# Weight tiles of 512 columns, the next pair's weights issued before this pair's products, three down rounds and 58 Strassen pairs in a two-block network on one core

## The chip, the core and the metric

The kernel runs on one core of a Trainium2 chip. The metric is the time of one execution in microseconds. TensorE (PE) multiplies, VectorE (DVE) and ScalarE (ACT) work on tiles in SBUF and empty PSUM, GpSimd (POOL) does little here, and SyncE (SP) issues nearly all loads.

## The reference

Sequences of 512 tokens with 1024 channels go through two models one after the other, two layers each, all in float32.

```python
for l in range(DEPTH):          # first model
    x = x + rms_norm(mixers(rms_norm(x, ...)) @ w_out[l], norm_mix_post[l])
    h = rms_norm(x, norm_mlp_pre[l])
    y = conv_mlp(h, w_up[l], conv_w[l], conv_b[l], w_down[l])
    x = x + rms_norm(y, norm_mlp_post[l])
# second model: 16 meta tokens are put ahead, 528 tokens
for l in range(DEPTH):
    h = h + 0.5 * swiglu(rmsnorm(h, g0), ffn_w_gate[l, 0], ffn_w_up[l, 0], ffn_w_down[l, 0])
    h = h + mixer(rmsnorm(h, g1), ...)
    h = h + 0.5 * swiglu(rmsnorm(h, g2), ffn_w_gate[l, 1], ffn_w_up[l, 1], ffn_w_down[l, 1])
def swiglu(x, w_gate, w_up, w_down):
    return (jax.nn.silu(x @ w_gate) * (x @ w_up)) @ w_down
```

Gate and up are 1024 x 2816, down is 2816 x 1024. The change touches the four `swiglu` blocks, and every weight load of the program.

## The kernel before

**Products.** Channels lie on partitions, tokens in columns. For float32 accuracy every operand is split into a high part (`whi`, `xh`) that ScalarE rounds and a low part (`wlo`, `xl`) that VectorE subtracts, and each product of 128 x 128 weights is three matmuls: high by high, high by low, low by high (`mm3`, L225 for 512 columns, L233 for halves of 256 and 272).

**Weights.** `wload` takes a tile of up to 1024 columns by a DMA on SP's queue (L191), then `wsplit` makes its high half on ScalarE (L202) and its low half on VectorE (L203). All weight tiles, `raw`, `sum`, `whi` and `wlo`, share 13 buffers of 1024 columns (`NW`).

**A feed-forward block** (`ffn2`) goes through 22 pairs of 128 gate rows and 128 up rows, m = 0 to 21. In a direct pair (m in `DIRECT`, and the first three of the first block) each of the two is a group of its own: 8 chunks of channels x 3 matmuls, in two halves of tokens for 528 tokens, so 48 matmuls a weight (tile `gu`). All other pairs, 66 in the four blocks, are done with seven products in place of eight (`strassen`): the gate's and the up's two halves of channels are a, b, c, d, VectorE makes four sums of weights (`pair`, L1001), and each product is 12 matmuls of 264 columns (256 in the last block, which has 512 tokens), 84 for a pair. They are named here by their weights: a, b, s2, s1, s3, d, s4. Three accumulators in two PSUM tiles (`yx` with Y and X, `z` with Z) are used over again:

```python
self.prod(Y, wg, 0, x1, a, True)        # a
nc.scalar.copy(pv[:, a], Y)             # L1041
self.prod(X, wg, 512, x2, a, True)      # b
tt(s[:, a], X, pv[:, a], ALU.add)       # L1039
self.prod(Y, w12, 512, fv, a, False)    # s2, goes on in Y
nc.scalar.copy(pv[:, b], Y)             # L1046
...
self.prod(Y, w34, 0, fu, b, False)      # s3, goes on in Y
nc.scalar.copy(v3[:, b], Y)             # L1052
```

Product d then goes on in Y, and s4 in Z. `strassen` is a generator: products d and s4 of a pair are emitted between products of the next one. `act` multiplies by the norm (L1091), takes silu (L1092), multiplies gate by up (L1093) and splits (L210, L211).

**Down.** After pair 11 (`NH` - 1) and after pair 21 the activations made so far go through the down weights: 8 outputs, each with 12 or 10 chunks (`dn`), added to the stream `xt` by VectorE (L1137). Two loads of 768 or 640 columns bring the weights of an output.

**Order.** The code is written in a program order. A scheduler with a table of costs then orders the instructions of each engine, with earlier ones first where several can run, and gives out the buffers; the order on each engine is fixed when the program is built. PSUM in this part is three tiles of two banks (`P`). Activations and temporaries use 63 buffers of 528 columns (`NSLOT`).

Of the kernel before, what the change touches and what calls it, by code (L numbers as in the profile page):

```python
# [22 lines left out]
NX = 512  # L23
# [12 lines left out]
NSLOT = 63  # L36
# [13 lines left out]
NW = 13  # L50
NH = 12
DIRECT = (0, 5, 9, 13, 18)
# [7 lines left out]
class Net:  # L60
# [30 lines left out]
    def begin(self, srcs, T, g):  # L91
# [13 lines left out]
        for k in range(0, NK, 2):  # L105
            for w in ws[:1]:
                self.wsplit(*w, slice(128 * k, 128 * k + 256))
            xs.append(self.xsplit(k, g(k), c))
            for w in ws[1:]:
                self.wsplit(*w, slice(128 * k, 128 * k + 256))  # L110
# [75 lines left out]
    def wload(self, src):  # L186
        if self.pre:
            return self.pre.pop(0)
        n = src.shape[-1]
        raw, hi, lo = self.wtiles()  # L190
        self.nc.sync.dma_start(raw[:, :n], src)  # L191
        self.wsplit(raw, hi, lo, slice(0, n))
        return hi, lo

    def wtiles(self):
        return self.wtile("raw", F32), self.wtile("whi"), self.wtile("wlo")

    def wtile(self, n, dt=F32R):
        return self.wp.tile([128, 1024], dt, tag="w", name=self.nm(n), bufs=NW)

# [13 lines left out]
    def mm3(self, ps, w, wc, xs, T, first, last, M=128, halves=(0, 1)):  # L214
# [6 lines left out]
        for i, (a, b) in enumerate(((wh, xh), (wh, xl), (wl, xh))):  # L221
            st, sp = first and i == 0, last and i == 2
            lh = a[:, wc : wc + M]
# [256 lines left out]
    def mixer1(self, l, xs):  # L480
# [441 lines left out]
    def mlp1(self, l, xs, next_g, tn):  # L922
# [22 lines left out]
        for m in range(NF):  # L945
# [27 lines left out]
        srcs = lambda m: [  # L973
            d["w_down"][l, m][:, 1024 * c : min(DFF, 1024 * c + 1024)] for c in range(3)
        ]
        for m in range(NK - 1):
# [4 lines left out]
            [srcs(NK - 1)], [(k // 8, 128 * (k % 8), k) for k in range(NF)], acts, ys, gcol, next_g, tn  # L981
        )

    def down(self, srcs, acts, T, p):
        k = 0
        for src in srcs:
            w = self.wload(src)
            for j in range(src.shape[-1] // 128):
                self.mm3(p[0], w, 128 * j, acts[k], T, k == 0, k == len(acts) - 1)
                k += 1  # L990
# [5 lines left out]
    def pair(self, gsrc, usrc):  # L996
# [3 lines left out]
        A, B = slice(0, 512), slice(512, 1024)  # L1000
        tt = lambda o, i, j, op: nc.vector.tensor_tensor(out=o, in0=i, in1=j, op=op)  # L1001
        wg, wu = self.wtiles(), self.wtiles()
        nc.sync.dma_start(wg[0], gsrc)
        nc.sync.dma_start(wu[0], usrc)
        w12, w34 = ((self.wtile("sum", F32), self.wtile("whi"), self.wtile("wlo")) for _ in range(2))
        g, u, s12, s34 = wg[0], wu[0], w12[0], w34[0]
        tt(s12[:, A], u[:, A], u[:, B], ALU.add)
        tt(s12[:, B], s12[:, A], g[:, A], ALU.subtract)
        tt(s34[:, A], g[:, A], u[:, A], ALU.subtract)
        tt(s34[:, B], g[:, B], s12[:, B], ALU.subtract)  # L1010
        self.wsplit(*wg, slice(0, 1024))
        self.wsplit(*w12, slice(0, 1024))
        self.wsplit(*w34, slice(0, 1024))
        self.wsplit(*wu, B)
        return [w[1:] for w in (wg, wu, w12, w34)]

    def prod(self, o, w, wc, xs, c, first):

        for k in range(NK // 2):
            l = slice(wc + 128 * k, wc + 128 * k + 128)  # L1020
# [6 lines left out]
    def strassen(self, gsrc, usrc, xs, T, rb, act):  # L1027
# [5 lines left out]
        wg, wu, w12, w34 = self.pair(gsrc, usrc)  # L1033
        x1, x2 = xs[: NK // 2], xs[NK // 2 :]
        fu, fv = zip(*self.forms)
        pa, pz = self.P("yx"), None
# [888 lines left out]
```

## Time and profile before

| | |
|---|---|
| median of 3 runs | 3728.61 us (3727.02 to 3731.86) |
| the profiled execution | 3724.06 us |
| its span, first to last instruction | 3722.3 us |
| busy: PE, DVE, ACT | 95%, 63%, 43% |
| mean granted TensorE clock | 0.985 |
| chain that ended last: PE, DVE, ACT, DMA | 80%, 12%, 4%, 3% of the span |

The rows of the profile give an engine's busy time, the count of instructions in brackets, and the idle time before an instruction with what ended it. Matmuls are pipelined, so their own durations overlap; the step from one start to the next tells the pace. The granted clock of 1.00 is the upper of TensorE's two levels, 2.4 GHz. The eight stretches of gate and up pairs begin at 1240, 1469, 2090, 2309, 2491, 2712, 3311 and 3529 us and take 1118 us together; down rounds, two mixers of each model and the convolution blocks fill the rest.

### The profile page before, as it was taken

Reading aid. Unit: us, or ns where it says so; the run is one execution under the profiler, and the core shown is the slowest. Engines: PE = TensorE matmul, PEld = TensorE weight load, DVE = VectorE, ACT = ScalarE, POOL = GpSimd, SP = SyncE. Lnnn points to the kernel's source line nnn. Section 1 sums busy time; section 2 is a strip of 40 time slices with the busy share of each in tenths; the row PEclk is TensorE's granted clock in tenths of the full one; section 3 lists DMA queues with packets and bytes.
Section 4 is the critical chain, followed back from the end, with each engine's and each line's share of the span. In section 5 each row is a group of like instructions: output and inputs, shape, how many; then the busy total and the mean of one; then the engine's idle time right before and its main releaser. Section 6 shows DMA issues by size and latency. Waiting matters only on the chain.

```text
span 3722.3 us, 57191 instructions
## 1 busy us (share of the span) xinstructions
PE 3554.3 (95%) x23315; PEld 3150.1 (85%) x23315; DVE 2352.6 (63%) x4340; ACT 1607.4 (43%) x2685; POOL 44.3 (1%) x184
## 2 busy tenths in 40 slices
PE   8999999999999899899999999898999999998988
PEld 6788888778888799898989989898999887778887
DVE  6767745777772774756546774777566664677475
ACT  3654433465442442434663442344334457344242
POOL 1000000000000000000000000000000000000000
PEclk9999999999999899999999999999999999999999
DMA  4213333212333133232112223232323212122322
GB/s 139 68 52 100 93 97 117 64 56 82 95 99 94 52 93 94 75 104 63 52 56 63 74 88 94 80 91 91 91 80 99 68 52 69 49 85 91 96 75 90
DMA packets 96278, 304.75 MB, mean 82 GB/s; under 512 B 11252, under 2 KB 15380, under 8 KB 96016
## 3 DMA queue, kind: packets, MB, share of 16 engines
q1 hardware_dynamic: 92016, 292.86, 26.1%
q0 software_dynamic: 2560, 6.93, 0.6%
q8 instruction: 183, 3.00, 0.3%
q10 hardware_dynamic: 1440, 1.32, 0.1%
q14 instruction: 79, 0.65, 0.1%
HBM read 298.97 MB, written 2.10 MB: 81 GB/s over the span
## 4 chain that ended last, share of the span: by engine, by line
PE 80%; DVE 12%; ACT 4%; DMA 3%; issue 2%; SPq 0%; DVEq 0%; ACTq 0%
PE up L225 12%; PE yx L1022 10%; PE dn L233 10%; PE dn L225 9%; PE g L233 7%; PE g L225 5%; PE gu L233 3%; DVE wlo L203 3%; DVE sum L1001 2%; PE z L1022 2%; PE wo L225 2%; DMA raw<-ffn_u 2%; PE pvd L555 1%; PE up L233 1%; PE wo L233 1%
## 5 line engine op out<-in xcount | busy, mean ns | idle before, releaser
L203 DVE TENSOR_TENSOR wlo<-raw,whi 128x1024 fp32r<-128x1024 f32 (+4 forms) x623 | 646.8, 1042 | 294.3 <-ACT whi L202 270.6
L202 ACT ACTIVATE whi<-raw 128x1024 fp32r<-128x1024 f32 (+4 forms) x623 | 564.6, 912 | 522.1 <-DMA raw<-w_down 121.6
L225 PE MATMUL up<-xh,whi 128*128 128x512 f32 x640 | 254.1, 397 | 0.0
L225 PE MATMUL up<-xh,wlo 128*128 128x512 f32 x640 | 252.4, 394 | 0.0
L225 PE MATMUL up<-xl,whi 128*128 128x512 f32 x640 | 251.2, 393 | 0.0
L233 PE MATMUL dn<-fal,whi 128*128 128x256 f32 (+1 forms) x1076 | 219.9, 284 | 0.0
L233 PE MATMUL dn<-fah,whi 128*128 128x256 f32 (+1 forms) x1076 | 219.8, 284 | 0.0
L233 PE MATMUL dn<-fah,wlo 128*128 128x256 f32 (+1 forms) x1076 | 219.3, 284 | 0.0
L1022 PE MATMUL yx<-xh,wlo 128*128 128x264 f32 (+1 forms) x528 | 156.8, 297 | 39.5 <-DVE wlo L203 39.5
L233 PE MATMUL g<-xh,whi 128*128 128x256 f32 (+1 forms) x848 | 185.9, 298 | 5.7 <-ACT ptm L1382 4.3
L1022 PE MATMUL yx<-xh,whi 128*128 128x264 f32 (+1 forms) x528 | 159.3, 302 | 23.5 <-ACT pv L1041 14.8
L233 PE MATMUL g<-xl,whi 128*128 128x256 f32 (+1 forms) x848 | 181.0, 289 | 0.2 <-DVE xl L277 0.2
L1137 DVE SCALAR_TENSOR_TENSOR xt<-dn,xt 128x528 f32<-128x528 f32 (+1 forms) x63 | 44.3, 703 | 215.3 <-PE dn L233 155.3
L233 PE MATMUL g<-xh,wlo 128*128 128x256 f32 (+1 forms) x848 | 179.7, 288 | 0.0
L1022 PE MATMUL yx<-fvh,whi 128*128 128x264 f32 (+1 forms) x528 | 157.9, 299 | 22.3 <-ACT v L1052 13.8
L202 ACT ACTIVATE whi<-sum 128x1024 fp32r<-128x1024 f32 x132 | 137.4, 1054 | 83.7 <-DVE wlo L203 19.4
L203 DVE TENSOR_TENSOR wlo<-sum,whi 128x1024 fp32r<-128x1024 f32 x132 | 158.8, 1219 | 19.6 <-ACT whi L202 11.1
L233 PEld LDWEIGHTS dn<-fal,whi 128*128 128x128 f32 x1076 | 169.1, 188 | 0.0
L233 PEld LDWEIGHTS dn<-fah,whi 128*128 128x128 f32 x1076 | 168.9, 188 | 0.0
L233 PEld LDWEIGHTS dn<-fah,wlo 128*128 128x128 f32 x1076 | 168.8, 188 | 0.0
L936 DVE SCALAR_TENSOR_TENSOR cc<-cu,v,cc 128x512 f32<-128x512 f32 x176 | 129.8, 749 | 41.4 <-ACT cc L934 38.7
L1022 PE MATMUL yx<-fvl,whi 128*128 128x264 f32 (+1 forms) x528 | 153.4, 291 | 0.0
(539 smaller groups left out, 9762.5 us busy)
## 6 DMA issues: line engine op xcount, KB each, us to landing
raw<-w_in SPq DMA_DIRECT2D x93, 512.0 KB, 3.6
raw<-w_up SPq DMA_DIRECT2D x88, 512.0 KB, 3.6
raw<-ffn_g SPq DMA_DIRECT2D x88, 512.0 KB, 3.6
raw<-ffn_u SPq DMA_DIRECT2D x88, 512.0 KB, 4.5
raw<-ffn_d SPq DMA_DIRECT2D x64, 384.0 KB, 3.2
raw<-ffn_d SPq DMA_DIRECT2D x64, 320.0 KB, 2.9
raw<-w_out SPq DMA_DIRECT2D x32, 512.0 KB, 3.6
raw<-w_down SPq DMA_DIRECT2D x32, 512.0 KB, 3.5
```

The lines of the kernel that those rows point to most:

```text
L202: self.nc.scalar.activation(hi[:, c], raw[:, c], AF.Copy)
L203: self.nc.vector.tensor_tensor(out=lo[:, c], in0=raw[:, c], in1=hi[:, c], op=ALU.subtract)
L225: nc.tensor.matmul(ps[:M, :], lhsT=lh, rhs=b[:, :NX], start=st, stop=sp)
L233: nc.tensor.matmul(o, lhsT=lh, rhs=b[:, c], start=st, stop=sp)
L555: nc.tensor.matmul(pv[b], lhsT=xs[k][a][:, tb], rhs=w[:, 512 * kk : 512 * kk + 512], start=k == 0 and i == 0, stop=k == NK - 1 and i == 2,)
L936: nc.vector.scalar_tensor_tensor(out=o[:, V], in0=u[:, s : s + NX], scalar=w(c), in1=o[:, V], op0=ALU.mult, op1=ALU.add)
L1001: tt = lambda o, i, j, op: nc.vector.tensor_tensor(out=o, in0=i, in1=j, op=op)
L1022: self.nc.tensor.matmul(o, lhsT=w[a][:, l], rhs=xs[k][b][:, c], start=first and k == 0 and i == 0, stop=k == NK // 2 - 1 and i == 2, skip_ ...
L1137: nc.vector.scalar_tensor_tensor(out=xv, in0=p[1], scalar=0.5, in1=xv, op0=ALU.mult, op1=ALU.add)
```

## The change

Weight tiles become units of 512 columns (`WU`), with buffers by kind: 6 `raw`, 3 `sum`, 9 `whi`, 9 `wlo`, 54 KB a partition where 52 KB were; `NSLOT` falls by one. `wload` brings and splits a tile unit by unit. In `ffn2`, `ahead` emits the loads, sums and splits of pair m + 1 before the products of pair m, unless a down round lies between. Down runs after pairs 7, 15 and 21. Seven pairs of a block are direct (`DIRECT`) where five were, so 58 pairs in place of 66 are done with seven products. The copies and sums of a pair go to the tiles `fg` and `fu` themselves, and `pv` and `v3` are gone.

```diff
-NSLOT = 63
+NSLOT = 62
-NW = 13
-NH = 12
-DIRECT = (0, 5, 9, 13, 18)
+WU = 512
+WB = {"raw": 6, "sum": 3, "whi": 9, "wlo": 9}
+ROUNDS = (8, 16, NF)
+DIRECT = (0, 3, 7, 11, 15, 18, 21)
...
-        n = src.shape[-1]
-        raw, hi, lo = self.wtiles()
-        self.nc.sync.dma_start(raw[:, :n], src)
-        self.wsplit(raw, hi, lo, slice(0, n))
-        return hi, lo
+        w = []
+        for c in range(0, src.shape[-1], WU):
+            n = min(WU, src.shape[-1] - c)
+            raw, hi, lo = (self.wtile(t) for t in ("raw", "whi", "wlo"))
+            self.nc.sync.dma_start(raw[:, :n], src[:, c : c + n])
+            self.wsplit(raw, hi, lo, slice(0, n))
+            w.append((hi, lo))
+        return tuple(zip(*w))
...
+        w = {"a": parts(a), "b": parts(b)}
+        s1 = sum_(c, d, ALU.add)
+        s2 = sum_(s1, a)
+        w["s2"] = parts(s2)
+        s3 = sum_(a, c)
+        w["s1"] = parts(s1)
+        s4 = sum_(b, s2)
+        w["s3"] = parts(s3)
+        w["d"] = parts(d)
+        w["s4"] = parts(s4)
+        return w
...
+        seven = lambda m: m < NF and not (m in DIRECT or done[2 * m : 2 * m + 2])
+        wp = {}
+        def ahead(m):
+            if m not in wp and seven(m):
+                wp[m] = self.pair(srcs[2 * m], srcs[2 * m + 1])
         for m in range(NF):
-            if not (m in DIRECT or done[2 * m : 2 * m + 2]):
-                cur = self.strassen(srcs[2 * m], srcs[2 * m + 1], xs, T, rb, act)
+            ahead(m)
+            if seven(m):
+                if seven(m + 1) and m + 1 not in ROUNDS:
+                    ahead(m + 1)
+                cur = self.strassen(wp.pop(m), xs, T, rb, act)
...
-            if m in (NH - 1, NF - 1):
+            if m + 1 in ROUNDS:
...
-                dsrc = lambda i: [dw[i][:, 128 * o + e * c : 128 * o + e * c + e] for c in range(2)]
+                dsrc = lambda i: dw[i][:, 128 * o : 128 * m + 128]
```

In the changed file the splits are L212 and L213, the sums of weights L1022, the copies of Y L1060, L1065 and L1071, VectorE's evacuations L1058, the matmuls of a pair L1042, and the loads L196 and L1012.

Three places in the order follow, all in the second feed-forward block at the first Strassen pair behind a direct pair. There the pair is `yx_3434` before and `yx_4354` after, the next one `yx_3452` and `yx_4380`.

ScalarE before, from the direct pair's silu to the third copy of Y:

```order
L1092 ACTIVATE fg_3418_20528<-fg_3418_20528 128x528
L210 ACTIVATE fah_3420_20534<-fg_3418_20528 128x528
L1041 COPY pv_3437_20567<-yx_3434_20564 128x264
L202 ACTIVATE whi_3441_20636<-raw_3440_20635 128x1024
L1046 COPY pv_3437_20567<-yx_3434_20564 128x264
L202 ACTIVATE whi_3447_20644<-sum_3446_20643 128x1024
L1052 COPY v3_3438_20568<-yx_3434_20564 128x264
```

And ScalarE after, the same stretch; `whi_4342` to `whi_4352` are s2, s1, s3, d and s4 of the next pair, `whi_4362` is a of the pair after it:

```order
L212 ACTIVATE whi_4342_22197<-sum_4341_22195 128x512
L220 ACTIVATE fah_4308_22129<-fg_4306_22123 128x528
L1060 COPY fg_4355_22222<-yx_4354_22221 128x264
L212 ACTIVATE whi_4345_22203<-sum_4340_22193 128x512
L212 ACTIVATE whi_4348_22209<-sum_4344_22201 128x512
L212 ACTIVATE whi_4350_22213<-raw_4335_22183 128x512
L212 ACTIVATE whi_4352_22217<-sum_4347_22207 128x512
L1065 COPY fg_4355_22222<-yx_4354_22221 128x264
L212 ACTIVATE whi_4362_22298<-raw_4358_22290 128x512
L1071 COPY fu_4356_22223<-yx_4354_22221 128x264
```

One split stood between two copies of the running pair, and now four, of half the width, stand between the first and the second and one between the second and the third.

VectorE before, from the end of the direct pair's work over the sum of X (`fg<-yx`) to the first use of Z:

```order
L203 TENSOR_TENSOR wlo_3427_20543<-raw_3425_20541,whi_3426_20542 128x512
L1093 TENSOR_TENSOR fg_3418_20528<-fg_3418_20528,fu_3419_20530 128x528
L211 TENSOR_TENSOR fal_3421_20535<-fg_3418_20528,fah_3420_20534 128x528
L1039 TENSOR_TENSOR fg_3435_20565<-yx_3434_20564,pv_3437_20567 128x264
L1001 TENSOR_TENSOR sum_3446_20643<-raw_3443_20638 128x512
L1001 TENSOR_TENSOR sum_3449_20646<-raw_3440_20635,raw_3443_20638 128x512
L1001 TENSOR_TENSOR sum_3446_20643<-sum_3446_20643,raw_3440_20635 128x512
L203 TENSOR_TENSOR wlo_3442_20637<-raw_3440_20635,whi_3441_20636 128x1024
L1001 TENSOR_TENSOR sum_3449_20646<-raw_3440_20635,sum_3446_20643 128x512
L203 TENSOR_TENSOR wlo_3448_20645<-sum_3446_20643,whi_3447_20644 128x1024
L1039 TENSOR_TENSOR fu_3436_20566<-z_3439_20608,v3_3438_20568 128x264
```

VectorE after, around the same sum of X; `wlo_4343` and `wlo_4346` are s2 and s1 of the next pair:

```order
L1112 TENSOR_TENSOR fg_4306_22123<-fg_4306_22123,fu_4307_22125 128x528
L213 TENSOR_TENSOR wlo_4343_22198<-sum_4341_22195,whi_4342_22197 128x512
L221 TENSOR_TENSOR fal_4309_22130<-fg_4306_22123,fah_4308_22129 128x528
L213 TENSOR_TENSOR wlo_4346_22204<-sum_4340_22193,whi_4345_22203 128x512
L1022 TENSOR_TENSOR sum_4347_22207<-raw_4333_22179,sum_4341_22195 128x512
L1058 TENSOR_TENSOR fg_4355_22222<-yx_4354_22221,fg_4355_22222 128x264
L213 TENSOR_TENSOR wlo_4349_22210<-sum_4344_22201,whi_4348_22209 128x512
L1022 TENSOR_TENSOR sum_4366_22306<-raw_4360_22294,raw_4361_22296 128x512
L1022 TENSOR_TENSOR sum_4367_22308<-sum_4366_22306,raw_4358_22290 128x512
L213 TENSOR_TENSOR wlo_4351_22214<-raw_4335_22183,whi_4350_22213 128x512
```

The next pair's sums and low halves stood behind the sum of X; now those of its first four units stand ahead of it.

TensorE before, at the start of product d of that pair (`whi_3426`, behind ten of twelve matmuls of the next pair's a):

```order
L1022 MATMUL yx_3452_20661<-xl_3252_19420,whi_3441_20636 128x264
L1022 MATMUL yx_3452_20661<-xh_3251_19419,wlo_3442_20637 128x264
L1022 MATMUL yx_3434_20564<-fvh_3266_19501,whi_3426_20542 128x264
L1022 MATMUL yx_3434_20564<-fvl_3267_19502,whi_3426_20542 128x264
L1022 MATMUL yx_3434_20564<-fvh_3266_19501,wlo_3427_20543 128x264
```

And TensorE after, at the start of d (`whi_4328`):

```order
L1042 MATMUL yx_4354_22221<-ful_4190_21451,whi_4326_22165 128x264
L1042 MATMUL yx_4354_22221<-fuh_4189_21450,wlo_4327_22166 128x264
L1042 MATMUL yx_4354_22221<-fuh_4206_21535,whi_4326_22165 128x264
L1042 MATMUL yx_4354_22221<-ful_4207_21536,whi_4326_22165 128x264
L1042 MATMUL yx_4354_22221<-fuh_4206_21535,wlo_4327_22166 128x264
L1042 MATMUL yx_4354_22221<-fvh_4157_21284,whi_4328_22169 128x264
L1042 MATMUL yx_4354_22221<-fvl_4158_21285,whi_4328_22169 128x264
L1042 MATMUL yx_4354_22221<-fvh_4157_21284,wlo_4329_22170 128x264
L1042 MATMUL yx_4380_22334<-xh_4149_21265,whi_4338_22189 128x264
```

Product d now follows s3 (`whi_4326`) with no other product between; the next pair's a was issued further up, in parts of 2, 7 and 3 matmuls behind s1, b and s2.

## Rows read from the trace of the kernel before

**Rows 1.** The page, busy time of TensorE: us, share of the span, instructions.

```profile
PE 3554.3 (95%) x23315; PEld 3150.1 (85%) x23315; DVE 2352.6 (63%) x4340; ACT 1607.4 (43%) x2685; POOL 44.3 (1%) x184
```

**Rows 2.** Busy time by stretch: length, then PE, PEld, DVE, ACT, POOL; granted clock, DMA.

```profile
1240.00:1399.60 159.60, 138.55 (x1058) 133.07 (x1057) 120.28 (x209) 72.05 (x122) 0.00 (x0) 0.95 0.24 70
1468.60:1595.40 126.80, 115.05 (x884) 111.18 (x883) 85.73 (x131) 48.84 (x76) 1.42 (x7) 0.97 0.27 84
2089.60:2240.90 151.30, 137.27 (x1083) 132.49 (x1082) 111.38 (x180) 63.90 (x100) 0.00 (x0) 1.00 0.26 81
2308.80:2435.00 126.20, 115.29 (x885) 111.33 (x884) 86.22 (x132) 48.74 (x76) 0.00 (x0) 0.97 0.27 82
2491.20:2643.70 152.50, 138.84 (x1083) 134.16 (x1081) 112.38 (x180) 63.58 (x99) 0.00 (x0) 0.99 0.26 80
2711.50:2837.30 125.80, 115.35 (x884) 111.38 (x883) 85.96 (x132) 48.74 (x76) 1.41 (x7) 0.97 0.27 84
3310.70:3465.00 154.30, 136.89 (x928) 125.59 (x927) 112.65 (x183) 64.30 (x100) 0.00 (x0) 0.97 0.25 79
3529.40:3650.90 121.50, 110.35 (x774) 102.11 (x774) 85.58 (x131) 49.15 (x77) 0.00 (x0) 0.97 0.27 86
```

**Rows 3.** Timeline, TensorE in a later pair: start, us, instruction, idle before and releaser.

```profile
2352.52 0.28 PE L1022 MATMUL yx<-xh,whi 128*128 128x264 f32 x1
2352.64 0.28 PE L1022 MATMUL yx<-xl,whi 128*128 128x264 f32 x1
2354.18 0.39 PE L1022 MATMUL yx<-xh,wlo 128*128 128x264 f32 x1 [1.25 <-DVE wlo L203]
...
2356.86 0.59 PE L1022 MATMUL yx<-fvh,whi 128*128 128x264 f32 x1 [1.20 <-ACT v L1052]
2357.25 0.42 PE L1022 MATMUL yx<-fvl,whi 128*128 128x264 f32 x1
2357.47 0.42 PE L1022 MATMUL yx<-fvh,wlo 128*128 128x264 f32 x1
```

**Rows 4.** Timeline in the first pair behind a direct pair.

```profile
2400.31 0.36 ACT L1041 COPY pv<-yx 128x264 f32<-128x264 f32 x1
...
2400.72 0.39 PE L1022 MATMUL yx<-xh,whi 128*128 128x264 f32 x1 [0.98 <-ACT pv L1041]
...
2402.54 0.43 DVE L1039 TENSOR_TENSOR fg<-yx,pv 128x264 f32<-128x264 f32 x1 [1.40 <-PE yx L1022]
...
2403.03 0.39 PE L1022 MATMUL yx<-fvh,whi 128*128 128x264 f32 x1 [0.59 <-DVE fg L1039]
```

**Rows 5.** Groups by shape, ScalarE: count, busy us, mean ns; idle before.

```profile
L202 ACT ACTIVATE whi<-raw 128x1024 fp32r<-128x1024 f32 x367 | 386.2, 1054 | 283.4 <-DMA raw<-w_down 105.2 <-DMA raw<-w_in 41.2 <-DMA raw<-ffn_g 29.4
L202 ACT ACTIVATE whi<-raw 128x512 fp32r<-128x512 f32 x98 | 61.7, 630 | 73.9 <-DMA raw<-w_pab 22.1 <-PE g L233 18.2 <-PE g L225 17.4
L1046 ACT COPY pv<-yx 128x264 f32<-128x264 f32 x49 | 18.4, 376 | 145.2 <-PE yx L1022 123.0 <-DVE sum L1001 22.2
```

**Rows 6.** Groups by shape, VectorE.

```profile
L203 DVE TENSOR_TENSOR wlo<-raw,whi 128x1024 fp32r<-128x1024 f32 x367 | 447.6, 1220 | 239.9 <-ACT whi L202 217.8 <-PE yx L1022 8.1 <-PE gu L233 6.7
L203 DVE TENSOR_TENSOR wlo<-raw,whi 128x512 fp32r<-128x512 f32 x98 | 67.1, 684 | 8.8 <-ACT whi L202 7.4
L1093 DVE TENSOR_TENSOR fg<-fg,fu 128x528 f32<-128x528 f32 x66 | 46.5, 704 | 13.2 <-ACT fg L1092 12.7
L1039 DVE TENSOR_TENSOR fg<-yx,pv 128x264 f32<-128x264 f32 x49 | 21.0, 429 | 39.5 <-PE yx L1022 39.5
```

**Rows 7.** Timeline, TensorE in a direct pair of the last block.

```profile
3545.24 0.40 PE L225 MATMUL gu<-xh,whi 128*128 128x512 f32 x1
3545.47 0.40 PE L225 MATMUL gu<-xl,whi 128*128 128x512 f32 x1
```

**Rows 8.** Waits of TensorE: who, for whom; us in total, times, longest.

```profile
PE yx L1022 <- DVE wlo L203: 39.5, 29, 2.0
PE gu L233 <- ACT gur L1086: 7.8, 1, 7.8
```

More of the change, by code (lines that the diff above doesn't have):

```diff
@@ L188, in wload, with wtile, wcol @@
             return self.pre.pop(0)
-        n = src.shape[-1]
-        raw, hi, lo = self.wtiles()
-        self.nc.sync.dma_start(raw[:, :n], src)
-        self.wsplit(raw, hi, lo, slice(0, n))
-        return hi, lo
-    def wtiles(self):
-        return self.wtile("raw", F32), self.wtile("whi"), self.wtile("wlo")
-    def wtile(self, n, dt=F32R):
-        return self.wp.tile([128, 1024], dt, tag="w", name=self.nm(n), bufs=NW)
+        w = []
[6 more added lines that the diff above has]
+        return tuple(zip(*w))
+    def wtiles(self):
+        return tuple([self.wtile(t) for _ in range(1024 // WU)] for t in ("raw", "whi", "wlo"))
+    def wtile(self, n):
+        return self.wp.tile([128, WU], F32 if n in ("raw", "sum") else F32R, tag=n, name=self.nm(n), bufs=WB[n])
+    @staticmethod
+    def wcol(w, c, n):
+        return w[c // WU][:, c % WU : c % WU + n]
     def wsplit(self, raw, hi, lo, c):
@@ L972, in mlp1 @@
         gcol = self.c1(l, 24)
-        srcs = lambda m: [
-            d["w_down"][l, m][:, 1024 * c : min(DFF, 1024 * c + 1024)] for c in range(3)
-        ]
+        srcs = lambda m: d["w_down"][l, m]
         for m in range(NK - 1):
@@ L980, in mlp1, with down @@
         return self.out1(
-            [srcs(NK - 1)], [(k // 8, 128 * (k % 8), k) for k in range(NF)], acts, ys, gcol, next_g, tn
+            [[srcs(NK - 1)]], [(0, 128 * k, k) for k in range(NF)], acts, ys, gcol, next_g, tn
         )
[L984 to L990, printed above, removed]
+    def down(self, src, acts, T, p):
+        n = len(acts)
+        for k in range(n):
+            if 128 * k % WU == 0:
+                w = self.wload(src[:, 128 * k : min(128 * k + WU, 128 * n)])
+            self.mm3(p[0], w, 128 * k % WU, acts[k], T, k == 0, k == n - 1)
     def c2(self, l, off):
@@ L999, in pair, with parts, sum_, prod @@
         nc = self.nc
[L1000 to L1017, printed above, removed]
+        C = slice(0, WU)
+        raw = []
+        for src in (gsrc, usrc):
+            for h in range(2):
+                raw.append(self.wtile("raw"))
+                nc.sync.dma_start(raw[-1], src[:, WU * h : WU * h + WU])
+        a, b, c, d = raw
+        def parts(t):
+            h, l = self.wtile("whi"), self.wtile("wlo")
+            self.wsplit(t, h, l, C)
+            return h, l
+        def sum_(i, j, op=ALU.subtract):
+            t = self.wtile("sum")
+            nc.vector.tensor_tensor(out=t, in0=i, in1=j, op=op)
+            return t
+        w = {"a": parts(a), "b": parts(b)}
[9 more added lines that the diff above has]
+        return w
+    def prod(self, o, w, xs, c, first):
         for k in range(NK // 2):
-            l = slice(wc + 128 * k, wc + 128 * k + 128)
+            l = slice(128 * k, 128 * k + 128)
             for i, (a, b) in enumerate(((0, 0), (0, 1), (1, 0))):
@@ L1025, in prod, with strassen @@
                 )
[L1027 removed]
+    def strassen(self, w, xs, T, rb, act):
         nc = self.nc
@@ L1142, in ffn2 @@
                 if fin and out is not None:
-                    self.ending(out, [self.wload(w) for w in dsrc(NK - 1)], acts)
+                    self.ending(out, self.wload(dsrc(NK - 1)), acts)
                 acts.clear()
```

55 lines of the change are left out of this document (27 added, 28 removed).

## The prediction

> **What bounds the kernel now.** I read the page's engine table first, then the busy time by stretch, then the timeline of two Strassen pairs, then the costs by shape. TensorE is busy for 95% of the span [rows 1], but its rows overlap, so the measure here is the step from one start to the next: 0.12 us for a product of 264 columns [rows 3], 0.23 us for one of 512 [rows 7]. The eight stretches of gate and up pairs (two to each of the four feed-forward blocks) are set against that step [rows 2]. In the six with 264 columns the length less 0.122 us per PE instruction is 30.5, 19.0, 19.2, 18.2, 20.4 and 18.0 us. In the last two the products have 256 columns (0.118 us by the ratio of columns) and the direct ones 512: 756 x 0.118 + 144 x 0.23 + 28 x 0.2 = 128, and 672 x 0.118 + 96 x 0.23 + 6 x 0.23 = 103, which leaves 26 and 19 us. Together TensorE loses 170 us. Some 8 us of it is one wait in the direct groups that open the first stretch [rows 8], which the change leaves. So **162 us are lost in 66 Strassen pairs, 2.45 us a pair.**
>
> Where it goes is seen in the timeline. In a pair that follows other Strassen pairs, TensorE stands after two products until the low half of the first weight tile is subtracted (1.25 us idle), then until a copy out of PSUM is done (1.20 us), and then the step is 0.22 us where it was 0.12: the granted clock is at its lower level, 1.2 GHz [rows 3]. In the first pair after a direct pair the waits are for evacuations: 0.98 us for the copy of Y, 0.59 us for the sum of X [rows 4]. The reason for the first kind is room and VectorE. A pair holds twelve of the thirteen 1024-column buffers, so the next pair's splits can't start early, and VectorE has more to do in a Strassen pair than TensorE: 3 splits x 1.22 + one half split 0.684 + 4 sums of the same 512 columns at that price + 5 evacuations x 0.43 + three 528-wide operations x 0.70 = 11.3 us [rows 6], against 84 x 0.122 = 10.25 us.
>
> **The change part by part.** *Weights a pair ahead, smaller units.* The order of the changed program shows it done: on VectorE the next pair's low halves stand before this pair's sum of X, where before they stood behind it. The 9 high and 9 low tiles hold the running pair's seven and two more, and each finished product frees one. A pair costs VectorE 4 x 0.684 + 7 x 0.684 + 5 x 0.43 + 2.1 = 11.8 us, 0.45 us more. A direct pair costs it 4 x 0.684 + 4 x 0.70 = 5.5 us beside 96 x 0.122 = 11.7 us of TensorE. Three Strassen pairs and a direct one are then 40.9 us of VectorE beside 42.4 us of TensorE; 1.3 pairs of lead carry the three. So I take the waits for weights, and the low clock that follows them, as gone.
>
> *What is late next.* The four handoffs of a pair: a, copy of Y, b, sum with X, s2, copy, s3, copy, d. TensorE's waits before [rows 4] show that b waits for the copy of Y and s2 for the sum. ScalarE now has splits of the next pair between these copies, and each split needs a buffer that one of this pair's products frees. I go through the first pair after a direct one by the new order, with 0.63 us for a split, 0.38 us for a copy [rows 5], and 0.1 us for each handover (an estimate: rows 4 show 0.05 us from the end of a copy to the product that waited for it, and TensorE's ends are modelled).
> a to b: one split, a 528-wide copy that waits for VectorE, and the copy come first, and 14 other products cover 1.71 us of 2.1: 0.4 us lost.
> b to s2: VectorE's queue (split 0.68, sum 0.68, then 0.43 us) passes the 7 products of cover by 0.25 us.
> s2 to s3: two splits wait for s2 and the next pair's a to free a buffer, then the copy: 2 x 0.63 + 0.38 + 0.3 = 1.95 us against 3 products of cover, 1.6 us lost.
> s3 to d: one split and the copy, 0.63 + 0.38 + 0.2 = 1.2 us, and nothing stands between.
> Sum 3.4 us. There are 15 such starts of a run (after a direct pair or a block's first group). At the 8 starts behind a down round, 8 and 3 products stand where 3 and 0 did, and I get 1.6 us in the same way. In the 35 later pairs the products of two pairs alternate, and only s3 to d stays uncovered, by about 0.5 us (bounds 0 and 1). Left over: 15 x 3.4 + 8 x 1.6 + 35 x 0.5 = 81 us; bounds 38 (half of the starts' price, later pairs 0) and 127 (4 us and 1 us).
>
> *Eight pairs made direct.* Six with 12 more products of 0.122 us (1.46 us), two in the last block with 48 x 0.23 - 84 x 0.118 = 1.2 us: 11 us, all on TensorE.
>
> *Three rounds of down.* The number of products stays. 32 more updates of xt, 0.70 us each on VectorE, lie beside 48 x 0.122 = 5.9 us of products per output, in which VectorE has two splits and one update, 2.1 us. I cost them at nothing; with that cover gone they are 22 us. The rounds now end on direct pairs, whose activation chain (three 528-wide operations of VectorE at 0.70, two of ScalarE at about 0.65 and the handovers, 4 us) lies beside the 42 products that need the earlier ones (5.1 us).
>
> *All other stages.* By the order there are 413 more weight splits outside the Strassen pairs. Two halves take 2 x 0.684 - 1.22 = 0.148 us more than one whole on VectorE, 61 us in all, and 2 x 0.63 - 1.054 = 0.206 us more on ScalarE, 85 us [rows 5, 6]. TensorE bounds these stages and waits for a low half only in the Strassen pairs [rows 8], so nearly all is hidden; I take 10 us (bounds -5 and 85), since the few short chains of the mixers get longer with them, and the last round before a feed-forward block has only 36 products per output beside its finishing work.
>
> The Trainium skill, VectorE: DVE Perf Modes, section on the TRN2 errata, speaks against smaller tiles: operations that read SBUF pay a fixed extra per instruction, a large tile once and many small ones each time, and it advises 512 elements or more. The rows above agree with the direction, and 512 stands on its limit. By that rule alone the 61 or 85 us would be the outcome and not the 10, which is the third rival below.
>
> **The sum.** The profiled execution takes 3724.1 us (span 3722.3). 3724 - 162 + 81 + 11 + 10 = 3664 us. The median of the runs is 4.5 us above the profiled one, so 3668 us.
>
> **The rivals.** (1) *The evacuations find their slots.* A split that runs a little earlier than I place it leaves the copies free, and every pair loses 0.2 us as a well-covered one: 12 us in place of 81, 3595 us, 3600 as a median. For it: in these stretches ScalarE is busy for 39 to 45% [rows 2]. Against: order is fixed, and a split that waits for a buffer holds the copy behind it.
> (2) *The handoffs cost each pair what I give to the first.* ScalarE's copies stand behind the next pair's splits in all 58 pairs: 58 x 3.4 = 197 us, 3724 - 162 + 197 + 21 = 3780 us, 3785 as a median, slower than before. It decides from (162 - 21) / 58 = 2.4 us a pair on. For it: VectorE is 96% full in a run of three, so a slip is not made good before the next direct pair. Against: in later pairs s4 and s1 of two pairs lie between s2 and s3.
> (3) *The fixed cost of each smaller instruction lands on the path* outside the pairs: 85 in place of 10 us, 3739 us, 3744 as a median, slower. Against: TensorE waits little for splits there [rows 8]. It is the rule of the skill told above.
> That the change does not do what it says is not a rival of weight: the order shows the splits ahead, and the counts of pairs are 66 and 58.
>
> **How the numbers follow.** The forecast has 0.57, rival 1 0.23, rival 2 0.10, rival 3 0.10. The forecast's own bounds are 3620 to 3715. The range reaches down to rival 1 at 3600 and up to 3725, which leaves half of rival 1 and most of rivals 2 and 3 outside, about 2 in 10. A measurement of this kernel tells 0.2% (7 us) from no change. Faster: the forecast and rival 1 whole, with the near ends of the others, 0.84; same 0.04; slower 0.12.
>
> **What would show it.** Right: the stretches of pairs lose some 80 us over the step, in waits of TensorE for L1060, L1065 and L1071 (copies) and L1058 (sums), hardly for low halves; the granted clock stays near 1.00 in them; the loss sits in the first pair of each run; the stages outside keep their lengths within a few us. Wrong: if waits of TensorE for low halves remain, VectorE's 96% was the bound and the lead too short; if the loss per pair is even along a run, it is rival 2; if the mixers or the convolution block grow by tens of us, it is rival 3.

## The result, and the profile after

The changed kernel takes 3672.32 us (median of 4 runs, 3670.6 to 3678.35), the kernel before beside it 3729.74 us: a ratio of 0.985, 95% interval 0.983 to 0.987. The forecast was 3668 us. The sum came out; the reason given for its largest term did not, as the experiments show.

The page of the changed kernel, busy time (to set beside [rows 1]):

```profile
PE 3543.5 (97%) x23303; PEld 3142.0 (86%) x23303; DVE 2412.7 (66%) x4863; ACT 1715.2 (47%) x3219; POOL 44.4 (1%) x184
```

Waits of TensorE: for what, us in total, times, longest (to set beside [rows 8]; no row for a low half in a pair is left):

```profile
PE yx L1042 <- ACT fu L1071: 20.1, 35, 0.9
PE yx L1042 <- ACT fg L1065: 14.9, 15, 1.0
PE gu L243 <- ACT gur L1105: 12.3, 1, 12.3
PE bc L388 <- DVE rs_y L375: 12.0, 6, 5.1
...
PE yx L1042 <- ACT fg L1060: 1.8, 2, 0.9
PE yx L1042 <- DVE fg L1058: 1.7, 3, 0.6
```

Five of the twelve stretches of pairs, three of which open a block: length, PE, PEld, DVE, ACT, POOL, granted clock, DMA share, GB/s (to set beside [rows 2]):

```profile
1251.00:1363.20 112.20, 93.80 (x717) 90.98 (x716) 83.78 (x166) 54.56 (x107) 0.00 (x0) 0.92 0.25 72
...
2088.70:2187.50 98.80, 91.46 (x731) 89.02 (x730) 75.70 (x139) 47.95 (x87) 0.00 (x0) 1.00 0.32 90
2234.20:2324.60 90.40, 87.53 (x698) 85.31 (x698) 70.89 (x121) 44.46 (x83) 0.00 (x0) 1.00 0.35 100
...
2474.70:2579.80 105.10, 94.29 (x730) 91.80 (x729) 80.17 (x146) 49.76 (x92) 0.00 (x0) 0.95 0.31 89
...
2764.30:2832.70 68.40, 65.97 (x530) 64.76 (x530) 48.03 (x83) 31.20 (x59) 1.41 (x7) 1.00 0.33 98
```

The stretches inside a block run at a clock of 1.00, where five of the eight stood at 0.97 [rows 2]; what is left at a lower clock lies at openings.

For this and all other kernels the **loss in the pairs** was measured directly: for every matmul of a seven-product pair the step from the start of the matmul before it, less 0.122 us (0.118 us at 256 columns), added up. Before it is 157.0 us, after it is 74.7 us. Matmuls that make the norm (`bc`) stand among those of some first pairs of a block, and the waits ahead of them are not in these sums; with them it is 161.4 us before, beside the 162 of the prediction, and 88.0 us after. By the place of the pair (us in all, without `bc`; number of pairs):

| | block opening | behind a direct pair | behind down | later in a run | all |
|---|---|---|---|---|---|
| before | 15.1 (4) | 44.4 (16) | 3.6 (4) | **93.9 (42)** | 157.0 (66) |
| after | 21.5 (4) | 29.0 (11) | 11.9 (8) | **12.2 (35)** | 74.7 (58) |

The four feed-forward blocks got 53 us shorter (10.8, 15.6, 9.2, 17.5), the two mixers of the second model 9 us, and the first model 10.6 us longer.

### The profile page after: what moved, and what is told of

Same layout as the page of the kernel before. It is cut to its first block, busy times and chain, and to the rows that moved or that the text cites. A ratio compares the mean times of both kernels' runs of the same rounds, so it can differ in the third digit from the quotient of the medians.

```text
span 3670.7 us, 60668 instructions
## 1 busy us (share of the span) xinstructions
PE 3543.5 (97%) x23303; PEld 3142.0 (86%) x23303; DVE 2412.7 (66%) x4863; ACT 1715.2 (47%) x3219; POOL 44.4 (1%) x184
## 5 line engine op out<-in xcount | busy, mean ns | idle before, releaser
L212 ACT ACTIVATE whi<-raw 128x512 fp32r<-128x512 f32 (+1 forms) x1078 | 662.8, 619 | 1132.1 <-PE dn L235 187.5
L213 DVE TENSOR_TENSOR wlo<-raw,whi 128x512 fp32r<-128x512 f32 (+1 forms) x1078 | 722.8, 672 | 465.4 <-ACT whi L212 450.6
L212 ACT ACTIVATE whi<-sum 128x512 fp32r<-128x512 f32 x232 | 145.5, 631 | 216.1 <-PE yx L1042 59.5
L213 DVE TENSOR_TENSOR wlo<-sum,whi 128x512 fp32r<-128x512 f32 x232 | 158.9, 688 | 57.3 <-ACT whi L212 54.0
L243 PE MATMUL gu<-xh,whi 128*128 128x256 f32 (+1 forms) x736 | 154.3, 290 | 14.4 <-ACT gur L1105 12.3
L1042 PE MATMUL yx<-fvh,whi 128*128 128x264 f32 (+1 forms) x464 | 138.7, 299 | 21.8 <-ACT fu L1071 20.1
L243 PE MATMUL gu<-xl,whi 128*128 128x256 f32 (+1 forms) x736 | 155.9, 288 | 1.2 <-DVE xl L287 1.2
L243 PE MATMUL gu<-xh,wlo 128*128 128x256 f32 (+1 forms) x736 | 155.3, 288 | 0.0
L235 PE MATMUL g<-xh,whi 128*128 128x512 f32 x344 | 146.3, 425 | 7.4 <-ACT xh L286 6.3
L243 PEld LDWEIGHTS g<-xh,whi 128*128 128x128 f32 (+1 forms) x848 | 132.8, 188 | 14.5 <-issue 7.1
```

The source lines that it names most:

```text
L212: self.nc.scalar.activation(hi[:, c], raw[:, c], AF.Copy)
L213: self.nc.vector.tensor_tensor(out=lo[:, c], in0=raw[:, c], in1=hi[:, c], op=ALU.subtract)
L235: nc.tensor.matmul(ps[:M, :], lhsT=lh, rhs=b[:, :NX], start=st, stop=sp)
L243: nc.tensor.matmul(o, lhsT=lh, rhs=b[:, c], start=st, stop=sp)
L1042: self.nc.tensor.matmul(o, lhsT=w[a][:, l], rhs=xs[k][b][:, c], start=first and k == 0 and i == 0, stop=k == NK // 2 - 1 and i == 2, skip_ ...
```

## The experiments

Ratios are to the kernel before on the same chip. "Lead" is the time from the issue of a pair's first weight load to the first matmul of its product a, median over the pairs.

| kernel | pairs | ratio, 95% interval | loss in pairs, us | later in a run, us | lead, us |
|---|---|---|---|---|---|
| before | 66 | 1 | 157.0 | 93.9 | 9.3 |
| g_first | 66 | 0.998 (0.997 to 0.999) | 149.9 | 70.7 | 9.3 |
| kinds1024 | 66 | 0.987 (0.985 to 0.988) | 108.4 | 34.3 | 20.4 |
| tight | 66 | 0.994 (0.992 to 0.996) | 120.1 | 56.8 | 14.5 |
| sums_first | 66 | 0.986 (0.985 to 0.987) | 84.6 | 25.4 | 24.7 |
| **units** | 66 | **0.982 (0.981 to 0.984)** | 80.8 | 23.1 | 27.8 |
| units_ahead | 66 | 0.986 (0.985 to 0.988) | 91.5 | 23.6 | 28.3 |
| no_ahead | 58 | 0.984 (0.982 to 0.985) | 68.2 | 10.6 | 30.8 |
| after | 58 | 0.985 (0.983 to 0.987) | 74.7 | 12.2 | 30.8 |
| direct5 | 66 | 0.989 (0.988 to 0.991) | 92.6 | 16.0 | 29.4 |
| rounds2d | 58 | 0.985 (0.983 to 0.986) | 76.4 | 11.2 | 28.8 |
| units_d4 | 70 | 0.985 (0.984 to 0.987) | 89.6 | 43.9 | 27.9 |
| units_d3 | 74 | 0.985 (0.983 to 0.987) | 97.7 | 52.0 | 27.7 |
| d3_pool | 74 | 0.990 (0.989 to 0.992) | 113.0 | 66.5 | 27.3 |

**Is it the order ahead?** The first kernel is the changed one without that order, the second has the units alone:

```diff
# no_ahead, from the changed kernel
-                if seven(m + 1) and m + 1 not in ROUNDS:
-                    ahead(m + 1)
# units: the same, and
-ROUNDS = (8, 16, NF)
-DIRECT = (0, 3, 7, 11, 15, 18, 21)
+ROUNDS = (12, NF)
+DIRECT = (0, 5, 9, 13, 18)
```

no_ahead. 

> The changed kernel (ratio 0.985) without the call that orders the next pair's weights: units of 512 columns, 58 pairs by seven and three down rounds stay. Theory (the order gives the gain): the low halves of a pair again stand behind the previous pair's sums on VectorE and its own first sum behind them, so TensorE waits for wlo again and each pair loses about what it lost before, 2.45 us: 58 x 2.45 = 142 us in place of the 81 measured, some 60 us more, 3730 us, ratio 1.00 (0.995 to 1.005), with waits of yx for wlo of 30 us and more and stretches at the lower clock. Rival A (smaller units give the gain: the first half tile is split in half the time, so TensorE waits half as long): 58 x 1.2 = 70 us, time as in the changed kernel, 3672 us, ratio 0.985. Rival B (the eight direct pairs relieve VectorE): also 0.985, and the loss of a run's later pairs is as small as in the changed kernel.

units. 

> Units of 512 columns with buffers by kind alone: the next pair's weights are not ordered ahead, direct pairs at 0, 5, 9, 13, 18 and two down rounds ending at 12 and 22, as in the kernel before. Theory (the order gives the gain): 66 pairs lose 2.45 us each as before, plus some 10 us elsewhere for the smaller splits: ratio 1.000 to 1.006, 3730 to 3752 us. Rival A (units give the gain): 66 x 1.2 = 80 us lost in place of 162, plus 10 elsewhere, less nothing: 3658 to 3670 us, ratio 0.983. If it lies between, the difference between this run and the run without the call ahead tells what direct pairs and rounds are worth by themselves.

My theory fell. Without the order ahead nothing comes back (0.984), and units alone, on the old direct pairs and rounds, are the fastest kernel of all (0.982, 3659.8 us; its interval just touches that of the changed kernel), with no wait for low halves. Rival A gave the right times, 80.8 us lost where it had 80; but "units" holds three things: buffers by kind, half-size tiles, and another order within a pair (a and b split ahead of the sums). The next four take them apart.

**Which part of the units?**

```diff
# g_first, from the kernel before: in pair(), ahead of the first sum
+        self.wsplit(*wg, slice(0, 1024))
         tt(s12[:, A], u[:, A], u[:, B], ALU.add)
# kinds1024, from the kernel before
-NW = 13
+WB = {"raw": 3, "sum": 2, "whi": 4, "wlo": 4}
-        return self.wp.tile([128, 1024], dt, tag="w", name=self.nm(n), bufs=NW)
+        return self.wp.tile([128, 1024], dt, tag=n, name=self.nm(n), bufs=WB[n])
# sums_first, from units: the four sums, then a, b, s1, s2, s3, s4, d split
-WB = {"raw": 6, "sum": 3, "whi": 9, "wlo": 9}
+WB = {"raw": 5, "sum": 4, "whi": 9, "wlo": 9}
# tight, from units
+WB = {"raw": 4, "sum": 3, "whi": 7, "wlo": 7}
```

g_first. 

> The kernel before with one line moved: the split of the gate tile (the weights of products a and b) stands ahead of the four sums of weights; tiles of 1024 columns and one pool of 13 stay. It asks why units alone gave the gain. Theory O (the order within a pair): in the kernel before, both loads of a later pair are issued at 2343.3 and 2345.8 us, VectorE waits for the second, makes four sums and then the low half that TensorE waits for; with the gate tile first, that low half needs the first load alone and is there some 4 us earlier. The 45 us that the first product loses at its low half go, 3725 - 45 = 3680 us, ratio 0.988 (0.983 to 0.993). Theories K (buffers by kind) and U (half-size tiles): the loads still come late and the sums stand later, so what product a gains products s1 and s2 lose, ratio 0.997 to 1.004.

kinds1024. 

> The kernel before with its 13 buffers of 1024 columns given out by kind: 3 for loaded weights, 2 for sums, 4 for high and 4 for low halves; order and size stay. Theory K (buffers by kind): with one pool of 13 and 12 tiles a pair, a load waits for a tile that a late product still reads; with loaded weights by themselves the third buffer is free when the gate tile of the pair before has been split, loads start several us earlier and the first product's wait goes, 45 us and up: ratio 0.980 to 0.990, with loads of the next pair issued before the products of the running one are half done. Theories O (order within the pair) and U (half-size tiles): 0.997 to 1.005, with the same waits of yx for wlo.

sums_first. 

> The kernel with units alone (ratio 0.982), with the order within a pair put back: all four sums of weights before the first split (5 buffers for loaded weights and 4 for sums in place of 6 and 3). Theory O: the low half of product a again stands behind four sums (4 x 0.69 us) that need all loads, waits for wlo return in the later pairs, about 1.2 us each: +50 to +70 us, ratio 0.995 to 1.000. Theories K and U: the loads come early enough that the sums are done in time, 0.980 to 0.985.

tight. 

> The kernel with units alone (ratio 0.982), with no buffer to spare over one pair: 4 for loaded weights, 7 for high and 7 for low halves in place of 6, 9 and 9. Theory K (spare buffers let the next pair's loads and splits start): without them each pair's weights wait for the products of the one before, so waits for wlo return, 1 to 2.5 us in each of 45 later pairs, and down rounds with fewer loads in flight lose too: ratio 0.993 to 1.005. Theories O and U (the small first piece is enough: only a's two halves have to come in time): 0.980 to 0.986.

Theory K holds. **The same 13 buffers of the same size, given out by kind, are worth 1.3%**, three quarters of units' gain. All of it comes in the pairs later in a run (34.3 us lost for 93.9); those behind a direct pair lose 55.1 us where they lost 44.4. The issues of loads on SP show why the later ones gain: start, us, load. First the kernel before, whose product a starts at 2352.52 [rows 3]:

```profile
2343.26 0.33 SPq L1003 DMA_DIRECT2D raw<-ffn_g  x1
2345.81 0.33 SPq L1004 DMA_DIRECT2D raw<-ffn_u  x1
```

Then kinds1024, where product a of the pair that these two bring starts at 2355.88 us:

```profile
2340.39 0.33 SPq L1003 DMA_DIRECT2D raw<-ffn_g  x1
2344.16 0.33 SPq L1004 DMA_DIRECT2D raw<-ffn_u  x1
```

```profile
2355.88 0.28 PE L1022 MATMUL yx<-xh,whi 128*128 128x264 f32 x1
```

9.3 us of lead became 15.5 here, 20.4 in the median. Who held the loads is in SP's waits of the kernel before (for what, us, times, longest): 41 of these 132 loads waited last for a split, with the largest sum, and 73 for a matmul. The largest row for a split, and the largest for a matmul of either load:

```profile
SPq L1003 <- DVE wlo L203: 425.5, 38, 18.6
SPq L1003 <- PE z L1022: 67.3, 15, 12.8
...
SPq L1004 <- PE yx L1022: 27.1, 15, 3.0
```

In kinds1024 no load of L1003 or L1004 waits for TensorE at all; nearly all wait for VectorE's splits (wlo, 106 times) and evacuations (24):

```profile
SPq L1003 <- DVE wlo L203: 340.7, 57, 15.5
SPq L1004 <- DVE wlo L203: 235.1, 49, 23.9
```

In one pool a load gets a tile that a late product may still read; a buffer for loaded weights is free as soon as its splits and sums are done. One thing is not held apart: kinds1024 runs the same instructions and SP issues its loads in the same order, but the scheduler orders the engines anew around other buffers, and more than a quarter of the instructions of ScalarE and VectorE stand elsewhere in their queues. So the 1.3% is that of the buffers with the order that they allow, and no run has one without the other. tight says the same from the other side: half-size tiles with no buffer to spare lose 39 us in the pairs against units. The order within a pair is worth 0.2% while loads come late. In g_first TensorE's waits (columns as above) moved; the first two rows were 13.8 and 2.4 us in the kernel before:

```profile
PE yx L1022 <- ACT v L1052: 47.1, 38, 2.8
PE yx L1022 <- ACT pv L1046: 22.9, 20, 1.3
...
PE yx L1022 <- DVE wlo L203: 6.6, 9, 0.8
```

39.5 us for low halves [rows 8] became 6.6, and the waits for the copies, L1052 above all, came in their place. In sums_first the order costs 0.4% against units, of which buffers (5 and 4 for 6 and 3) may be a part. kinds1024 and sums_first, much alike but for the size, differ by less than their intervals: half size saves 24 us in the pairs, 20 of them behind direct pairs (55.1 to 35.5), and gives back 15, since the first model takes 7 us more and the first mixer of the second model 8; the spans differ by 3 us, so some 6 us more go elsewhere.

**What does the order ahead do, then?**

```diff
# units_ahead, from the changed kernel: its order, and the old constants
-ROUNDS = (8, 16, NF)
-DIRECT = (0, 3, 7, 11, 15, 18, 21)
+ROUNDS = (12, NF)
+DIRECT = (0, 5, 9, 13, 18)
```

> The kernel with units alone (ratio 0.982), with the next pair's weights ordered ahead of this pair's products as in the changed kernel; direct pairs at 0, 5, 9, 13, 18 and two down rounds stay. Theory (the two spare buffers of a kind already bring the next pair's weights early enough, so the order ahead only puts seven splits in front of copies and sums of a first pair): it costs some 0.1 us in each of 66 pairs as in the step from the run without the call (3666) to the changed kernel (3670): 3660 + 4 to + 8 us, ratio 0.983 to 0.984; the rest of the 26 us between this kernel and the run with five direct pairs is then that of three down rounds. Rival (the order ahead and runs of four pairs do not go together, since VectorE has no time left): 3675 to 3686 us, ratio 0.987 to 0.990. Second rival (it helps where VectorE is not short): 0.980.

It costs 0.4%, between the first theory and its rival; in the pairs 10.7 us. The lead of the loads is the same, 28.3 and 27.8 us, and the loss sits where the prediction saw a price: 16 first pairs lose 42.3 us where they lost 34.1, openings 2 us more. ScalarE around the third copy of a first pair, start, us, instruction; first units, then the changed kernel:

```profile
2334.01 0.63 ACT L212 ACTIVATE whi<-raw 128x512 fp32r<-128x512 f32 x1 [1.70 <-PE yx L1042]
2334.54 0.36 ACT L1065 COPY fg<-yx 128x264 f32<-128x264 f32 x1
2334.80 0.63 ACT L212 ACTIVATE whi<-sum 128x512 fp32r<-128x512 f32 x1
```

```profile
2286.11 0.63 ACT L212 ACTIVATE whi<-raw 128x512 fp32r<-128x512 f32 x1 [1.69 <-PE yx L1042]
2286.65 0.61 ACT L212 ACTIVATE whi<-sum 128x512 fp32r<-128x512 f32 x1
2287.16 0.36 ACT L1065 COPY fg<-yx 128x264 f32<-128x264 f32 x1
```

One more split stands ahead of the copy, 0.5 us, and product s3 waits for it: in such a pair it loses 0.8 us in units and 1.3 us in units_ahead and the changed kernel.

**Direct pairs and rounds.**

```diff
# direct5, from the changed kernel
+DIRECT = (0, 5, 9, 13, 18)
# rounds2d, from the changed kernel
+ROUNDS = (11, NF)
+DIRECT = (0, 3, 7, 10, 14, 18, 21)
# units_d4, units_d3, from units
+DIRECT = (0, 6, 11, 17)
+DIRECT = (0, 8, 15)
```

direct5. 

> The changed kernel with the direct pairs at 0, 5, 9, 13, 18 as before: 66 pairs by seven, weights ahead, three down rounds ending at 8, 16, 22. Eight pairs by seven for eight direct ones save 11 us of products. Theory (VectorE has just enough time in a run of three pairs, 11.8 us of work beside 10.3 us of products, so the direct pair is needed): runs of four, and runs that a down round cuts, fall further behind; the fourth pairs (4 to 6 in a block) wait 2 to 4 us, +30 to +50 us, and the time is 3690 to 3710 us, ratio 0.990 to 0.995. Rival (the direct pairs are not needed, the order alone does it): 3672 - 11 - about 10 for fewer starts of a run = 3650 us, ratio 0.979.

It was slower than the changed kernel by 0.4%, toward the theory, but not for its reason. Fourth pairs don't fall behind: later pairs lose 16.0 us in 38. The five more first pairs cost 13.5 us and the openings 4.1, less the 11 us of products; that is half of the 13 us between the two spans (3683.9 and 3670.7). The pair ahead of a down round, no longer a direct one, is now finished in front of it, and the down rounds of a block take 1 us more; the rest is open.

rounds2d. 

> The changed kernel with two down rounds of 11 products' depth (ending at 11 and 22) in place of three of 8, 8 and 6; direct pairs at 0, 3, 7, 10, 14, 18, 21, so still 58 pairs by seven. Theory (the block openings lose 17 us more than before since the last round, six chunks deep, leaves VectorE behind when the next block's first group starts): with eleven chunks each output has 66 products (8.1 us) for the same work of VectorE, the openings lose what they lost before, and 4 starts behind a down round go, 1.44 us each: 3672 - 17 - 6 = 3650 us, ratio 0.979; the first waits of a block (bc, gu) as in the kernel before. Rival (the openings lose for another reason: the new order or the smaller splits, not the depth of the last round): 3672 - 6 = 3666 us, ratio 0.983. Second rival (eleven chunks hold more slots, so the split activations of the later pairs wait for slots): slower than 0.985.

Inconclusive in its sum, clear in its parts. The third block, which follows a last round directly, got 8 us shorter (392.7 to 384.7 us), with TensorE's waits for the norm (`bc`) 5.6 us where the changed kernel has 12.0:

```profile
PE bc L388 <- DVE rs_y L375: 5.6, 5, 2.4
```

So the shallow last round does cost the next opening, but once, not 17 us over all (with `bc`, that block's first pair loses 13.2 us in the changed kernel and 3.1 here); and 4 starts behind down became starts behind a direct pair at 2.6 us for 1.5. The first two theories were each half right.

units_d4. 

> The kernel with units alone, with direct pairs at 0, 6, 11, 17 in place of 0, 5, 9, 13, 18: 70 pairs by seven, runs of five and four. Theory (VectorE is no limit, since the third and fourth pair of a run lose 0.3 us): four direct pairs less save 4 x 1.4 = 6 us of products and four starts of a run at 2.2 us, 9 us: 3660 - 15 = 3645 us, ratio 0.978. Rival (VectorE needs the direct pair to catch up: 11.8 us of work beside 10.3 us of products in each pair): the fifth pairs wait 3 us and more and the opening of the next run too, 3665 us and more, ratio 0.983 or above.

units_d3. 

> The kernel with units alone, with direct pairs at 0, 8, 15: 74 pairs by seven, runs of seven and six that the down round behind pair 11 cuts once. Theory (VectorE is no limit): 3660 - 8 x 1.4 - 8 x 2.2 = 3631 us, ratio 0.975. Rival (VectorE falls behind by 1.5 us in each pair): from the fifth pair of a run on each loses 1.5 us, some 24 pairs, 36 us: 3631 + 36 = 3667 us, ratio 0.985.

Both are slower than units, as the rivals said, and again not as they said: no loss grows along a run. Inside a long run every pair but the last two loses the same 1.4 to 1.5 us, nearly all at d, and the next starts 11.4 to 11.6 us later. TensorE, then ScalarE, then VectorE there in units_d3:

```profile
2145.44 0.28 PE L1042 MATMUL yx<-xh,wlo 128*128 128x264 f32 x1
2146.83 0.39 PE L1042 MATMUL yx<-fvh,whi 128*128 128x264 f32 x1 [1.10 <-ACT fu L1071]
2147.05 0.28 PE L1042 MATMUL yx<-fvl,whi 128*128 128x264 f32 x1
2147.18 0.29 PE L1042 MATMUL yx<-fvh,wlo 128*128 128x264 f32 x1
```

```profile
2145.34 0.64 ACT L220 ACTIVATE fah<-fg 128x528 fp32r<-128x528 f32 x1 [0.47 <-DVE fg L1112]
2145.89 0.61 ACT L212 ACTIVATE whi<-raw 128x512 fp32r<-128x512 f32 x1
2146.41 0.36 ACT L1071 COPY fu<-yx 128x264 f32<-128x264 f32 x1
```

```profile
2143.41 0.68 DVE L1022 TENSOR_TENSOR sum<-raw,raw 128x512 f32<-128x512 f32 x1
2144.01 0.68 DVE L213 TENSOR_TENSOR wlo<-raw,whi 128x512 fp32r<-128x512 f32 x1
2144.61 0.70 DVE L1112 TENSOR_TENSOR fg<-fg,fu 128x528 f32<-128x528 f32 x1
2145.23 0.68 DVE L213 TENSOR_TENSOR wlo<-sum,whi 128x512 fp32r<-128x512 f32 x1
```

s3 is done some 2 us before, but its copy stands on ScalarE behind the split of the pair before (`fah`), which waits for VectorE's product L1112, which stands behind the next pair's sums and splits. A direct pair takes 96 x 0.122 = 11.7 us, a seven-product pair in the middle of a run 11.4 to 11.6: so it saves next to nothing against a direct one, and 70 or 74 pairs by seven gain nothing over 66.

**Is that pace VectorE's work?** Two of the four sums go to GpSimd:

```diff
# d3_pool, from units_d3 (sum_ takes the engine as an argument)
-        s3 = sum_(a, c)
+        s3 = sum_(a, c, eng=nc.gpsimd)
...
-        s4 = sum_(b, s2)
+        s4 = sum_(b, s2, eng=nc.gpsimd)
```

> The run with direct pairs at 0, 8, 15 and units alone (ratio 0.985), with two of the four sums of weights in each pair (a - c and b - s2) on GpSimd in place of VectorE. In that run each pair inside a long run loses 1.4 us and starts 11.5 us after the one before, VectorE 92% busy. Theory (VectorE's work sets that pace): 1.4 us of it go, the pace of inner pairs falls toward the 10.25 us of the products; some 24 inner pairs gain 1.0 us each: 3666 - 24 = 3642 us, ratio 0.978. Rival (the pace is the handoff from s3 to d, a copy of ScalarE behind the next pair's splits): nothing changes there, 0.984 to 0.986. Second rival (sums on GpSimd take long or slow VectorE down while both run, so s3 and s4 come late): slower than 0.987.

The second rival came true: 0.990. Groups by shape of d3_pool: count, busy us, mean ns; idle before:

```profile
L1022 POOL TENSOR_TENSOR sum<-raw,raw 128x512 f32<-128x512 f32 x74 | 115.9, 1566 | 978.2 <-DMA raw<-ffn_u 497.3 <-DVE wlo L213 473.0 <-DVE fu L1058 7.9
L1022 POOL TENSOR_TENSOR sum<-raw,sum 128x512 f32<-128x512 f32 x74 | 100.2, 1354 | 551.3 <-DVE wlo L213 551.3
```

```profile
L213 DVE TENSOR_TENSOR wlo<-raw,whi 128x512 fp32r<-128x512 f32 x1000 | 713.4, 716 | 443.1 <-ACT whi L212 430.7 <-PE sc L1386 2.8 <-PE dsc L771 1.9
L1022 DVE TENSOR_TENSOR sum<-raw,raw 128x512 f32<-128x512 f32 x74 | 51.0, 690 | 50.2 <-POOL sum L1022 49.1 <-DMA raw<-ffn_u 0.9
```

A sum takes 1.35 to 1.57 us there for VectorE's 0.69, and VectorE's own sums wait 49 us for GpSimd's. So inner pairs lose 1.8 us, and whether less work on VectorE would set a faster pace stays open.

## Why the prediction was right, and where it was not

- **The 162 us before and the 81 us left over.** The pairs lose 157.0 and 74.7 us, or 161.4 and 88.0 us with the waits for `bc`, which the prediction's way of counting included: 82 or 73 us came back for a forecast of 81. The waits left are those named: copies L1071 and L1065.
- **The cause was credited to the wrong edit.** The step that failed is the first one, "weights a pair ahead, smaller units": I read in the order that low halves stand ahead of the sums, and took that as what brings the weights. The prediction's own sentence on room (12 of 13 buffers in a pair) was the cause: by kind, 13 buffers free the loads, and the order ahead adds a loss in the pairs of 6.5 us (after against no_ahead) to 10.7 (units_ahead against units). The sum came out all the same because the changed kernel holds both edits and the forecast priced what was left over, not which of them brings the weights; that part is luck. The issue of each load against its first product would have shown it beforehand: 9.3 us, of which a landing (3.6 us, the median of the gate loads), four sums of 0.68 us, a split (1.05) and its low half (1.22) leave next to nothing.
- **The terms inside the 81.** Starts of a run: forecast 15 x 3.4 = 51 us, measured 50.5, which is luck too. 12 of them, behind a direct pair and at the first block's opening, lose 2.6 us each (the chain by hand was right in s2 to s3 and s3 to d, about 1.3 and 1.1 us for 1.6 and 1.2, while a to b and b to s2 cost 0.1); the other three openings lose 5.8, 5.5 and 7.6 us, which I had not told apart. Behind down 8 x 1.49 (forecast 1.6), later 35 x 0.35 (forecast 0.5).
- **VectorE's 11.8 us in a pair was too much.** Its rows overlap: in the rows of units_d3 above, operations of 0.68 us start every 0.61 us. In that kernel it is busy 21.25 us in two inner pairs, 10.6 us each. In the changed kernel's stretch from 2234.20, six such pairs and two direct ones, it is busy for 70.9 of 90.4 us. So "96% full in a run of three", the case for direct pairs, did not hold; a direct pair more costs little for another reason, the even pace above.
- **Direct pairs and rounds.** Products +11 us as forecast; from units to no_ahead the pairs lose 12.6 us less, and the whole step costs 0.2%, within the intervals. The opening behind six chunks is a term that I named ("only 36 products") and gave no price of its own: 8 us.
- **Other stages, forecast 10 us.** The spans differ by 51.6 us; with 82 back in the pairs and 11 given to direct products, 20 us went elsewhere. The first model took 10.6 us more, the second model's mixers 9 less, and the four blocks outside the pairs' steps 18 more, of which 9 are waits for `bc` (12.0 us, 2.8 before) and 4.5 the wait for `gur` (12.3 us, 7.8 before [rows 8]). The start of the second model's blocks (1232.6 us before, 1236.7 in kinds1024, 1245.0 in units, 1243.2 in the changed kernel) puts some 7 to 8 us on the smaller splits. The fixed price of an instruction is there: a split of 512 columns takes VectorE 0.684 us and one of 1024 columns 1.220 [rows 6]. The Trainium skill states such a price per instruction for operations of VectorE that read SBUF (VectorE: DVE Perf Modes, section on the TRN2 errata), and the trace agrees. But rival 3, all 85 us of it on the path, did not come.

## What to carry to other kernels

Before crediting an order, measure each load's lead over its first use, and ask which buffer it waited for: one pool for tiles of short and long life makes the short ones wait for the long, and giving the same memory out by kind brought most of the gain here. Once loads come early, more work ordered ahead only stands in front of the copies that free PSUM. When a change bundles several edits, run the plainest alone: here units without the rest beat the kernel before by 1.8% and the changed one by 0.3%, the latter at the edge of the intervals.

## What the runs showed of the hardware that I had not expected

- Operations of VectorE and ScalarE that follow without a gap start closer than they last: 0.61 us for 0.68 (VectorE, 128x512), 0.54 and 0.51 for 0.63 and 0.61 (ScalarE splits and the copy behind, rows of the changed kernel above). Adding durations overstates a full engine by a tenth or more.
- A single wait of 1.1 us before d is followed by one step of 0.22 us and then by 0.13 and 0.12 (units_d3: 2146.83, 2147.05, 2147.18, 2147.30), where two waits 2.7 us apart were followed by one step of 0.39 and 12 of 0.22 [rows 3]. The granted clock was 1.00 behind the single wait (2146.80 to 2149.00) and 0.69 on average behind the two (2357.20 to 2361.50 in the kernel before).
- While GpSimd makes sums, VectorE's split takes 716 ns where it took 687 in units_d3, 4% more:

```profile
L213 DVE TENSOR_TENSOR wlo<-raw,whi 128x512 fp32r<-128x512 f32 x1000 | 685.1, 687 | 441.0 <-ACT whi L212 423.0 <-PE sc L1386 2.8 <-ACT rbc L411 2.0
```

The Trainium skill (GPSIMD Engine Reference, section 1, Specifications) says that GpSimd shares its SBUF interfaces with VectorE, with contention when an instruction of VectorE has two inputs in SBUF, as a split has; the 4% fits that. Its section 4.1 puts an operation with two inputs at about twice VectorE's time; the sums, 1.35 and 1.57 us for 0.69, agree.
